# Seven-product weight pairs: second chunk split first, the first unit's copies dealt out, other pairs in units 2 and 3

## The chip, the cores and the metric

The kernel runs on one core of a Trainium2 chip. The metric is the device time of one execution in microseconds (us). The core has five engines, each with its own instruction queue: TensorE (PE in the profile) multiplies matrices into PSUM, VectorE (DVE) and ScalarE (ACT) work on elements, GpSimd (POOL) does some element work and issues accumulating DMAs, SyncE (SP) issues the loads of the weights. Engines wait for one another by semaphores, and each takes its instructions in the order in which they were written to it.

## The reference

The model is a trunk of two layers over 256 tokens of width 2048, all in float32. Layer 0 mixes tokens by attention (16 query heads, 4 key heads), layer 1 by a recurrent block. After each mixer comes a gated feed-forward of width 5632, and this is what the change touches:

```
x = x + mixer(rms_norm(x, norm_mix[i]))
x = x + swiglu(rms_norm(x, norm_ffn[i]), w_gate[i], w_up[i], w_down[i])

def swiglu(h, w_gate, w_up, w_down):
    return (silu(h @ w_gate) * (h @ w_up)) @ w_down
```

## The kernel before, in words

**Precision.** Each float32 weight chunk (128 x 1024) is split in two reduced-precision parts: ACT casts it to "hi" and DVE subtracts, giving "lo". A product of an activation block and a weight block is then three matmuls of 128 x 512: activation hi by weight hi, activation lo by weight hi, activation hi by weight lo (`product`, L323, L324 and L326). The last of the three is the first that needs "lo".

**Units.** The gate and up projections of a feed-forward are cut into 11 units of 512 features (numbered 0 to 10 in the code; the text calls them unit 1 to 11). A unit goes through the 2048 rows of the weights in eight pairs, 0 to 7, of 256 rows. Each pair is two chunks in DRAM: one of the gate weights, one of the up weights, 512 KB each. Within a chunk lie two blocks of 128 rows x 512 features. With the two halves of the tokens, a pair is a 2 x 2 by 2 x 2 block product.

**Plain pairs and seven-product pairs.** A plain pair forms its eight block products (`wide`, 24 matmuls). A seven-product pair forms seven (21 matmuls) from sums of blocks, in the manner of Strassen's and Winograd's scheme. Its weight operands are b11 and b21 (the two blocks of the first chunk), t1 = b11 + b12 and b22 (in the second chunk), t2 = t1 + b22, t3 = t2 - b11 and t4 = b21 + t2. Matching sums of the activations (`Norm.form`) are made once for each feed-forward. `SEVEN` names the pairs treated so in most units, `FEWER` the exceptions in units 1 to 3.

**Preparing a seven-product pair** (`load_seven`, from L149). Two loads land in "raw" tiles. t1 is made in place: on DVE (L174) when the three loads ahead of it are plain ones (`soon`), otherwise by an accumulating DMA that POOL issues (L176) once both chunks have landed. Then the inner function `two` casts a whole chunk on ACT (L163) and subtracts on DVE (L164). `combine` makes t2, t3 and t4 in place in the raw tiles (DVE, L169) and casts them (ACT, L170, "ohi" for t2 and "hi" for t3 and t4), and three remainders follow (DVE, L171, "olo" for t2). In a plain pair `load_half` does the cast (L145) and the remainder (L146).

**Order.** PE's order is written out by hand. The other engines' orders come from a planner that simulates a timeline, with added rules: `behind("cast", ...)` chains all casts on ACT in program order, and `behind("rest", ...)` chains the remainders and sums on DVE. `follow` and `ahead` add single rules of that kind. Buffers limit how far the preparation can run ahead: 8 raw tiles and 7 pairs of hi and lo tiles, of which a seven-product pair takes three.

**The end of a unit.** `sums` (L769 to L773) combines four of the products in PSUM, L791 to L795 add the rest and apply SiLU and the product of gate and up. DVE then transposes 32 x 32 blocks (L408) and 16 small copies (L416, 404 ns each on ACT) move them into place. A cast (L801) and a remainder (L802) make the operand of the down projection. With `beside`, the 16 copies aren't issued at once: they are put in four portions on the list `tail`, the last with L801 and L802, and each following `load_seven` issues one. Without it all 16 follow at once. Before the change unit 1 and the last unit are without it. The tiles "one" and "two" have one buffer each, so a unit's `sums` come after all portions of the unit before it.

**Neighbours.** Units 1 and 2 follow each other directly, then unit 3; from there on two down projections (`wide_project`, plain chunks) stand between units. Unit 1 follows the mixer's output projection, whose last PSUM banks DVE adds to x at L347.

Of the kernel before, what the change touches and what calls it, by code (L numbers as in the profile page):

```python
# [12 lines left out]
F32 = mybir.dt.float32  # L13
F32R = mybir.dt.float32r
AF = mybir.ActivationFunctionType
ALU = mybir.AluOpType
AX = mybir.AxisListType

P = 128
# [8 lines left out]
PARTS = [8, 8, 8, 8, 12]  # L28
UNIT = 4
SEVEN = (0, 1, 2, 4, 5, 6)  # L30
FEWER = {0: (0, 5, 6), 1: (4, 5, 6), 2: (1, 4, 5, 6)}
HALF = 8
CHUNK = HALF * P
WIDE = 512
# [40 lines left out]
def trunk(ctx, tc, w, out):  # L75
    nc = tc.nc
    act, dve, pool, pe, sync = nc.scalar, nc.vector, nc.gpsimd, nc.tensor, nc.sync
# [11 lines left out]
    def nm(s):  # L89
        uid[0] += 1  # L90
        return f"{s}_{uid[0]}"

    def tmp(tag, shape=(P, S), dt=F32, bufs=2):
        pl = tp if tag in COMMON else scope[-1]
        return pl.tile(list(shape), dt, tag=tag, name=nm(tag), bufs=bufs)
# [4 lines left out]
    def follow(i, j):  # L100
        tc.add_manual_dep(
            i.ins, j.ins.name,
            mybir.DependencyInfo(mybir.DependencyClass.NoSync, mybir.DependencyReason.DATA),
            reason="order",
        )
# [12 lines left out]
    def landing(shape):  # L118
        n = used[0] = (used[0] + 1) % (RING + RAWS)
        if ft and n >= RING:  # L120
            return scope[-1].tile(shape, F32, tag="xraw", name=nm("raw"), bufs=RAWS)
        return wp.tile(shape, F32, tag="raw", name=nm("raw"), bufs=RING)

    def behind(key, i):
        if key in newest:
            follow(i, newest[key])
        newest[key] = i
        for rule in [rule for rule in ahead if key == rule[2]]:
            rule[0] -= 1
            if rule[0] == 0:  # L130
                follow(i, rule[1])
                ahead.remove(rule)
# [21 lines left out]
    def load_seven(srcs, soon):  # L154
        raw = [landing([P, 2, WIDE]) for _ in range(2)]
        for r, src in zip(raw, srcs):
            sync.dma_start(out=r, in_=src)
        (b11, b21), (t1, b22) = ([r[:, j, :] for j in range(2)] for r in raw)
        got = {}

        def two(src, names):
            hi, lo = parts([P, 2, WIDE])
            behind("cast", act.copy(hi, src))  # L163
            behind("rest", dve.tensor_tensor(lo, src, hi[:].bitcast(F32), ALU.subtract))  # L164
            for j, name in enumerate(names):
                got[name] = hi[:, j, :], lo[:, j, :]

        def combine(o, x, y, op, hi, lo):
            behind("rest", dve.tensor_tensor(o, x, y, op))  # L169
            behind("cast", act.copy(hi, o))  # L170
            return lambda: behind("rest", dve.tensor_tensor(lo, o, hi.bitcast(F32), ALU.subtract))  # L171

        if soon:
            behind("rest", dve.tensor_tensor(t1, b11, t1, ALU.add))  # L174
        else:
            pool.dma_start(out=t1, in_=b11, accum_op=ALU.add)  # L176
        two(raw[0], ("b11", "b21"))
        two(raw[1], ("t1", "b22"))
        if tail:
            tail.pop(0)()  # L180
        one = [tmp(t, (P, WIDE), F32R) for t in ("ohi", "olo")]
        hi, lo = parts([P, 2, WIDE])
        got["t2"] = tuple(one)
        got["t3"], got["t4"] = ((hi[:, j, :], lo[:, j, :]) for j in range(2))
        t2 = b22
        rests = [
            combine(t2, t1, b22, ALU.add, *got["t2"]),
            combine(b11, t2, b11, ALU.subtract, *got["t3"]),
            combine(b21, t2, b21, ALU.add, *got["t4"]),
        ]  # L190
        while parted:
            follow(parted.pop(), newest["cast"])
        for rest in rests:
            rest()
        return got
# [21 lines left out]
    def ffn_order(l):  # L217
        seq = []
        for what, i in ffn_plan():
# [3 lines left out]
            both = [(w[f"w_gate{l}"][i, c], w[f"w_up{l}"][i, c]) for c in range(KT // 2)]  # L223
            seq += sum(([b] if c in (FEWER.get(i, SEVEN)) else list(b) for c, b in enumerate(both)), [])
        return seq + out_order(w[f"w_down{l}_{len(PARTS) - 1}"], UNIT // 2)
# [524 lines left out]
    def ffn(norm, nxt):  # L750
        def bank():
            return ps_m.tile([P, 2 * S], F32, tag="pm", name=nm("pm"))

        def unit(seven, beside, engines, soon):
            xs, r = norm.xs, [norm.r[:, a : a + 1] for a in range(2)]
            m1, p5, p6, p7 = (bank() for _ in range(4))
            c11, c21, c12, c22 = (new_acc() for _ in range(4))
            new = [m1, p5, p7, p6, c11, c21, c12, c22]

            def fresh(o):  # L760
                n = len(new)
                new[:] = [b for b in new if b is not o]
                return len(new) < n

            one, h = (tmp(n, (P, 2, WIDE), bufs=1) for n in ("one", "two"))
            (base, u), (v, x) = ([t[:, a, :] for a in range(2)] for t in (one, h))

            def sums():
                follow(act.copy(base, m1), newest["cast"])  # L769
                dve.tensor_tensor(u, base, p6, ALU.add)  # L770
                dve.tensor_tensor(v, u, p5, ALU.subtract)
                dve.tensor_tensor(u, u, p7, ALU.add)
                ahead.append([2, dve.tensor_tensor(x, u, p5, ALU.subtract), "rest"])  # L773

            for c in range(KT // 2):
                if c not in seven:
                    for pair in ((c11, c21), (c12, c22)):
                        wide(pair, xs, 2 * c, KT, [fresh(o) for o in pair])
                        if pair[0] is c11 and c == seven[-1] + 1:
                            sums()  # L780
                    continue
                wt, end = half(), c == seven[-1]
                n1, n3, n2, n4 = norm.forms[c]
                a11, a12, a22 = block(xs, 2 * c, 0), block(xs, 2 * c + 1, 0), block(xs, 2 * c + 1, 1)
                for o, y, b in (
                    (m1, a11, "b11"), (c11, a12, "b21"), (p5, n1, "t1"), (c12, n4, "b22"),
                    (p6, n2, "t2"), (p7, n3, "t3"), (c21, a22, "t4"),
                ):
                    product(o, y, wt[b], fresh(o), end and any(o is m for m in (m1, p5, p7, p6)))
            for o, y, b in ((base, base, c11), (u, u, c21)):  # L790
                features = dve.tensor_tensor(o, y, b, ALU.add)  # L791
            for a, (o, y, b) in enumerate(((base, v, c12), (u, x, c22))):
                table_act(o, o, AF.Silu, scale=r[a])
                last = dve.tensor_tensor(y, b, y, ALU.subtract)  # L794
            dve.tensor_tensor(h, h, one, ALU.mult)  # L795
            ahead.extend([[1 if soon else 3, features, "rest"], [2 if soon else 4, last, "rest"]])
            t, ht = act_four(), turn_blocks(h, engines, h, tail if beside else None)

            def whole(move=list):
                move()  # L800
                act.copy(t[:, :, :S], ht)  # L801
                dve.tensor_tensor(t[:, :, S:], ht, t[:, :, :S].bitcast(F32), ALU.subtract)  # L802

            if beside:
                tail.append(partial(whole, tail.pop()))
            else:
                whole()
            return [t[:, k, :] for k in range(UNIT)]

        hid = [[] for _ in PARTS]  # L810
        ends = np.cumsum(PARTS) // UNIT
        for what, i in ffn_plan():
            if what == "unit":
                hid[int(np.searchsorted(ends, i, "right"))] += unit(FEWER.get(i, SEVEN), 0 < i < ends[-1] - 1, (act,) if i < ends[-1] - 1 else (act, dve), i < ends[0])
            else:
                for a, acc in enumerate(wide_project(hid[i[0]], PARTS[i[0]], bank)):
                    t = tmp("form", (P, WIDE))
                    m = act.activation(t, acc, AF.Copy, scale=norm.r[:, a : a + 1])
                    if i[1] % 2:
                        parted.append(m)  # L820
                    pool.dma_start(out=x_tm[:, a, i[1] * WIDE : (i[1] + 1) * WIDE], in_=t, accum_op=ALU.add)
        if nxt is not None:
            ln_exp_tables()
        groups(hid[-1], PARTS[-1], PARTS[-1] - UNIT, lambda: None, partial(add_residual, norm=nxt, store=nxt is None, scale=norm.r))
        scope.pop()
        ft.pop().close()
# [216 lines left out]
```

## Time and profile before

| | |
|---|---|
| median of 3 runs | 1952.77 us (1952.69 to 1953.58) |
| profiled execution | 1952.89 us |
| its span, first to last instruction | 1951.1 us |
| PE busy | 1938.0 us (99%), 9224 matmuls |
| DVE busy | 1768.6 us (91%) |
| ACT busy | 1448.3 us (74%) |
| POOL busy | 401.3 us (21%) |
| loads from HBM | 382.13 MB |
| accumulating DMAs for t1 (L176) / sums on DVE (L174) | 90 / 26 |
| chunks of seven-product pairs (L163) | 232, so 116 pairs |
| first feed-forward's units | 266.39 us to about 884 us |
| second feed-forward's units | 1263.38 us to about 1881 us |

A row of the timeline has the start in us from the start of the span, the duration in us, engine, line, operation, the tile written and the tiles read, shapes and count. In brackets stands how long the engine sat idle ahead of it and what ended that. A matmul's row has a duration that overlaps with the next one's, so its cost has to be read from the distance of two starts.

### The profile page before, as it was taken

Reading aid. Unit: us, or ns where it says so; the run is one execution under the profiler, and the core shown is the slowest. Engines: PE = TensorE matmul, PEld = TensorE weight load, DVE = VectorE, ACT = ScalarE, POOL = GpSimd, SP = SyncE. Lnnn points to the kernel's source line nnn. Section 1 sums busy time; section 2 is a strip of 40 time slices with the busy share of each in tenths; the row PEclk is TensorE's granted clock in tenths of the full one; section 3 lists DMA queues with packets and bytes.
Section 4 is the critical chain, followed back from the end, with each engine's and each line's share of the span. In section 5 each row is a group of like instructions: output and inputs, shape, how many; then the busy total and the mean of one; then the engine's idle time right before and its main releaser. Section 6 shows DMA issues by size and latency. Waiting matters only on the chain.

```text
span 1951.1 us, 27630 instructions
## 1 busy us (share of the span) xinstructions
PE 1938.0 (99%) x9224; PEld 1624.0 (83%) x9224; DVE 1768.6 (91%) x2417; ACT 1448.3 (74%) x2358; POOL 401.3 (21%) x497
## 2 busy tenths in 40 slices
PE   9999999999999999999999999999999999999999
PEld 8898888788888888888899998887888888888887
DVE  7878698999999999998799997898999999999993
ACT  7677686777777777777698887866778776787772
POOL 0442250011101111010465450520101111011100
PEclk9999999999999999999999999999999999999999
DMA  8434746698878978787365556555878888788872
GB/s 328 156 127 152 248 158 197 196 272 236 248 233 243 262 240 246 235 244 246 126 223 188 189 164 245 175 194 174 253 236 248 245 248 253 231 246 251 246 257 86
DMA packets 131727, 426.42 MB, mean 219 GB/s; under 512 B 14720, under 2 KB 14976, under 8 KB 131584
## 3 DMA queue, kind: packets, MB, share of 16 engines
q1 hardware_dynamic: 108944, 383.21, 58.0%
q0 software_dynamic: 22496, 41.43, 11.9%
q8 instruction: 72, 1.18, 0.2%
q14 instruction: 71, 0.58, 0.1%
q10 hardware_dynamic: 144, 0.02, 0.0%
HBM read 382.13 MB, written 2.10 MB: 197 GB/s over the span
## 4 chain that ended last, share of the span: by engine, by line
PE 92%; DVE 4%; ACT 1%; issue 1%; DMA 1%; POOL 0%; SPq 0%; ACTq 0%; DVEq 0%; POOLq 0%
PE acc L326 14%; PE acc L323 14%; PE acc L324 14%; PE pm L326 11%; PE pm L323 11%; PE pm L324 11%; PE acc L294 8%; PE acc L292 4%; PE pm L306 1%; PE pm L307 1%; PE pm L305 1%; DVE lo L146 1%; ACT hi L145 1%; DVE lo L164 0%; DMA raw<-in_w_in_dram 0%
## 5 line engine op out<-in xcount | busy, mean ns | idle before, releaser
L146 DVE TENSOR_TENSOR lo<-raw,hi 128x1024 fp32r<-128x1024 f32 (+1 forms) x474 | 574.5, 1240 | 77.1 <-ACT hi L145 75.3
L145 ACT CAST hi<-raw 128x1024 fp32r<-128x1024 f32 (+1 forms) x474 | 478.4, 1045 | 116.5 <-PE acc L324 72.1
L326 PE MATMUL acc<-lo,xg 128*128 128x512 f32 x744 | 290.9, 391 | 2.0 <-DVE lo L146 1.8
L323 PE MATMUL acc<-hi,xg 128*128 128x512 f32 x744 | 290.0, 390 | 0.0
L324 PE MATMUL acc<-hi,xg 128*128 128x512 f32 x744 | 289.6, 389 | 0.0
L164 DVE TENSOR_TENSOR lo<-raw,hi 128x1024 fp32r<-128x1024 f32 x232 | 275.0, 1217 | 6.5 <-ACT hi L163 3.8
L294 PE MATMUL acc<-xg,hi 128*128 128x512 f32 x832 | 271.7, 397 | 0.6 <-ACT hi L145 0.6
L163 ACT CAST hi<-raw 128x1024 fp32r<-128x1024 f32 x232 | 234.6, 1048 | 41.0 <-issue 14.4
L176 POOL DMA_DIRECT2D raw<-raw x90 | 77.7, 863 | 903.9 <-DVE raw L174 369.5
L323 PE MATMUL pm<-hi,act 128*128 128x512 f32 x512 | 199.2, 389 | 0.0
L324 PE MATMUL pm<-hi,act 128*128 128x512 f32 x512 | 199.2, 389 | 0.0
L326 PE MATMUL pm<-lo,act 128*128 128x512 f32 x512 | 199.2, 389 | 0.0
L416 ACT COPY two<-one 32x256 f32<-32x256 f32 x420 | 169.7, 404 | 24.7 <-DVE one L408 16.5
L292 PEld LDWEIGHTS acc<-xg,lo 128*128 128x128 f32 x832 | 156.3, 188 | 35.4 <-DVE lo L146 2.8
L323 PE MATMUL acc<-hi,act 128*128 128x512 f32 x448 | 174.9, 390 | 0.4 <-DVE two L794 0.4
L326 PE MATMUL acc<-lo,act 128*128 128x512 f32 x448 | 174.4, 389 | 0.0
L324 PE MATMUL acc<-hi,act 128*128 128x512 f32 x448 | 174.4, 389 | 0.0
L292 PE MATMUL acc<-xg,lo 128*128 128x256 f32 x832 | 171.8, 281 | 1.2 <-DVE lo L146 1.2
L326 PEld LDWEIGHTS acc<-lo,xg 128*128 128x128 f32 x744 | 139.7, 188 | 34.1 <-DVE lo L146 5.4
L324 PEld LDWEIGHTS acc<-hi,xg 128*128 128x128 f32 x744 | 139.7, 188 | 29.2
L323 PEld LDWEIGHTS acc<-hi,xg 128*128 128x128 f32 x744 | 139.7, 188 | 28.6
L170 ACT CAST hi<-raw 128x512 fp32r<-128x512 f32 x232 | 137.1, 622 | 32.8 <-DVE raw L169 31.8
(221 smaller groups left out, 3852.1 us busy)
## 6 DMA issues: line engine op xcount, KB each, us to landing
raw<-in_w_gate_dram SPq DMA_DIRECT2D x176, 512.0 KB, 4.6
raw<-in_w_up_dram SPq DMA_DIRECT2D x176, 512.0 KB, 5.5
raw<-in_w_down_dram SPq DMA_DIRECT2D x176, 512.0 KB, 4.4
raw<-in_w_in_dram SPq DMA_DIRECT2D x64, 512.0 KB, 4.4
raw<-raw POOLq DMA_DIRECT2D x90, 256.0 KB, 5.8
raw<-in_w_q_dram SPq DMA_DIRECT2D x32, 512.0 KB, 3.8
raw<-in_w_o_dram SPq DMA_DIRECT2D x32, 512.0 KB, 4.2
x<-form POOLq DMA_DIRECT2D x64, 256.0 KB, 6.7
```

The source lines that it names most:

```text
L145: behind("cast", act.copy(hi[:, sl], raw[:, sl]))
L146: behind("rest", dve.tensor_tensor(lo[:, sl], raw[:, sl], hi[:, sl].bitcast(F32), ALU.subtract))
L163: behind("cast", act.copy(hi, src))
L164: behind("rest", dve.tensor_tensor(lo, src, hi[:].bitcast(F32), ALU.subtract))
L170: behind("cast", act.copy(hi, o))
L176: pool.dma_start(out=t1, in_=b11, accum_op=ALU.add)
L292: pe.matmul(acc[:, S:], w, xs[k][:, :S], start=False, stop=stop)
L294: pe.matmul(acc, w, xs[k], start=(k == 0), stop=stop)
L323: pe.matmul(o, xh, wh, start=start, stop=False)
L324: pe.matmul(o, xl, wh, start=False, stop=False)
L326: pe.matmul(o, xh, wl, start=False, stop=stop)
L416: m = (eng.copy if eng is act else eng.tensor_copy)(to[:, :, :, i, :], of[:, :, :, j, :])
```

## The change

In `load_seven` the second chunk (t1, b22) is cast and split first. The sum t2 is made right behind it, ahead of the cast and remainder of the first chunk (b11, b21). The cast of t2 comes behind the first chunk's cast, and only then the portion of copies from `tail`. On PE the products that use t1 and b22 go first, then those with b11 and b21. Unit 1 gets `beside`, so its 16 copies are dealt out in four portions. Unit 2 has the pairs 2, 4, 5, 6 as seven-product pairs in place of 4, 5, 6; unit 3 has 2, 4, 5, 6 in place of 1, 4, 5, 6. The number of seven-product pairs becomes 118.

```diff
-FEWER = {0: (0, 5, 6), 1: (4, 5, 6), 2: (1, 4, 5, 6)}
+FEWER = {0: (0, 5, 6), 1: (2, 4, 5, 6), 2: (2, 4, 5, 6)}
...
             pool.dma_start(out=t1, in_=b11, accum_op=ALU.add)
+        two(raw[1], ("t1", "b22"))
+        one = [tmp(t, (P, WIDE), F32R) for t in ("ohi", "olo")]
+        t2 = b22
+        behind("rest", dve.tensor_tensor(t2, t1, b22, ALU.add))
         two(raw[0], ("b11", "b21"))
-        two(raw[1], ("t1", "b22"))
+        behind("cast", act.copy(one[0], t2))
         if tail:
             tail.pop(0)()
-        one = [tmp(t, (P, WIDE), F32R) for t in ("ohi", "olo")]
         hi, lo = parts([P, 2, WIDE])
         got["t2"] = tuple(one)
         got["t3"], got["t4"] = ((hi[:, j, :], lo[:, j, :]) for j in range(2))
-        t2 = b22
         rests = [
-            combine(t2, t1, b22, ALU.add, *got["t2"]),
+            lambda: behind("rest", dve.tensor_tensor(one[1], t2, one[0].bitcast(F32), ALU.subtract)),
             combine(b11, t2, b11, ALU.subtract, *got["t3"]),
             combine(b21, t2, b21, ALU.add, *got["t4"]),
         ]
...
                 for o, y, b in (
-                    (m1, a11, "b11"), (c11, a12, "b21"), (p5, n1, "t1"), (c12, n4, "b22"),
+                    (p5, n1, "t1"), (c12, n4, "b22"), (m1, a11, "b11"), (c11, a12, "b21"),
                     (p6, n2, "t2"), (p7, n3, "t3"), (c21, a22, "t4"),
                 ):
...
-                hid[...] += unit(FEWER.get(i, SEVEN), 0 < i < ends[-1] - 1, (act,) if i < ends[-1] - 1 else (act, dve), i < ends[0])
+                hid[...] += unit(FEWER.get(i, SEVEN), i < ends[-1] - 1, (act,) if i < ends[-1] - 1 else (act, dve), i < ends[0])
```

In the last line the index of `hid` is cut.

More of the change, by code (lines that the diff above doesn't have):

```diff
@@ L813, in ffn @@
             if what == "unit":
-                hid[int(np.searchsorted(ends, i, "right"))] += unit(FEWER.get(i, SEVEN), 0 < i < ends[-1] - 1, (act,) if i < ends[-1] - 1 else (act, dve), i < ends[0])
+                hid[int(np.searchsorted(ends, i, "right"))] += unit(FEWER.get(i, SEVEN), i < ends[-1] - 1, (act,) if i < ends[-1] - 1 else (act, dve), i < ends[0])
             else:
```

## The prediction

> **What bounds the kernel now.** I read the page's head first, then TensorE's (PE's) own rows for its pace, then PE counted by stretches, and last the rows of VectorE (DVE) and ScalarE (ACT) where PE falls behind.
>
> ```profile
> span 1951.1 us, 27630 instructions
> PE 1938.0 (99%) x9224; PEld 1624.0 (83%) x9224; DVE 1768.6 (91%) x2417; ACT 1448.3 (74%) x2358; POOL 401.3 (21%) x497
> PE 92%; DVE 4%; ACT 1%; issue 1%; DMA 1%; POOL 0%; SPq 0%; ACTq 0%; DVEq 0%; POOLq 0%
> ```
>
> PE holds 92% of the chain of waits, DVE 4%. The change can gain by fewer matmuls or where PE waits. PE rows at the first feed-forward's start:
>
> ```profile
> 266.39 0.39 PE L323 MATMUL pm<-hi,xg 128*128 128x512 f32 x1
> 266.62 0.39 PE L324 MATMUL pm<-hi,xg 128*128 128x512 f32 x1
> ...
> 267.07 0.39 PE L323 MATMUL acc<-hi,xg 128*128 128x512 f32 x1
> ...
> 267.52 0.39 PE L326 MATMUL acc<-lo,xg 128*128 128x512 f32 x1
> ```
>
> Five steps take 1.13 us: a matmul costs 0.2267 us (rounded times, over longer stretches), though each row says 0.39, since they overlap. So a plain pair (24 matmuls) is 5.44 us of PE, a seven-product pair (21) 4.76.
>
> PE counted by stretches (us, busy and count, clock, DMA share, GB/s):
>
> ```profile
> 270.00:330.00 60.00, 60.00 (x266) 1.00 0.58 184
> ...
> 340.00:356.00 16.00, 15.16 (x65) 1.00 0.63 216
> 356.00:392.00 36.00, 34.67 (x149) 1.00 0.62 194
> ...
> 1337.00:1353.00 16.00, 15.14 (x65) 1.00 0.63 216
> 1353.00:1389.00 36.00, 34.66 (x149) 1.00 0.61 194
> ```
>
> At full pace 60 us hold 60/0.2267 = 264.7, and the count has 1.3 more because it takes in matmuls begun earlier. At that pace 16 us would hold 71.9 and 36 us 160.1. PE is 6.9 and 11.1 short: 1.56 us lost around the end of the second unit, 2.52 us in the third, 4.08 us in each feed-forward and 8.2 us in both. The clock is full, so this is waiting.
>
> Why PE is late there, in ACT's and DVE's rows:
>
> ```profile
> 320.76 6.64 ACT L416 COPY two<-one 32x256 f32<-32x256 f32 x16 [1.11 <-DVE one L408]
> ```
> ```profile
> 308.68 5.76 DVE L146 TENSOR_TENSOR lo<-raw,hi 128x1024 fp32r<-128x1024 f32 x5
> 314.35 1.21 DVE L795 TENSOR_TENSOR two<-two,one 128x1024 f32<-128x1024 f32 x1
> ...
> 317.76 0.68 DVE L174 TENSOR_TENSOR raw<-raw,raw 128x512 f32<-128x512 f32 x1
> ...
> 328.08 0.69 DVE L171 TENSOR_TENSOR olo<-raw,ohi 128x512 fp32r<-128x512 f32 x1 [4.19 <-ACT ohi L170]
> ...
> 337.22 2.35 DVE L164 TENSOR_TENSOR lo<-raw,hi 128x1024 fp32r<-128x1024 f32 x2
> 339.61 0.69 DVE L169 TENSOR_TENSOR raw<-raw 128x512 f32<-128x512 f32 x1
> 340.33 1.29 DVE L169 TENSOR_TENSOR raw<-raw,raw 128x512 f32<-128x512 f32 x2
> 341.55 0.69 DVE L171 TENSOR_TENSOR olo<-raw,ohi 128x512 fp32r<-128x512 f32 x1
> 342.15 1.29 DVE L171 TENSOR_TENSOR lo<-raw,hi 128x512 fp32r<-128x512 f32 x2
> 343.35 1.22 DVE L146 TENSOR_TENSOR lo<-raw,hi 128x1024 fp32r<-128x1024 f32 x1
> ...
> 1325.07 0.69 DVE L171 TENSOR_TENSOR olo<-raw,ohi 128x512 fp32r<-128x512 f32 x1 [4.19 <-ACT ohi L170]
> ```
>
> The first unit's 16 copies run as one block of 6.64 us on ACT, ahead of the cast "ohi", and DVE stands 4.19 us for it, in both feed-forwards. One seven-product pair takes DVE from 337.22 to 343.35, 6.13 us, against PE's 4.76; a plain pair takes two of five chunks in 5.76, 2.30 us, against 5.44. Each seven costs DVE's lead 1.4 us and each plain pair returns 3.1: DVE sets the pace where sevens stand close.
>
> **Part 1, one more seven in the second unit.** Three matmuls fewer in each feed-forward: 3 x 0.2267 = 0.68 us, 1.36 in both. By the 0.39 of the rows it would be 2.34; I take the starts. The Trainium skill (Perfetto Trace Analysis, Tensor Engine Instruction) has a matmul's reported end as an estimate from its size, not an observation; by that rule too the 0.39 is no cost, and the spacing of the starts bears it out.
>
> For DVE the pair costs 6.13 - 2.30 = 3.83 us more. The sum of pair 4 (0.61 of DVE, one step of such rows) leaves for a POOL accumulate, since a seven now stands three loads ahead; pair 2 takes one instead. Nothing in balance in unit 2; in unit 3 one sum is gone.
>
> **Part 2, the first unit's copies dealt out.** Four copies (1.65 us of ACT) go behind each of the four sevens, so DVE's 4.19 us go. With part 1: 3.83 - 4.19 = -0.36 us for DVE up to the end of pair 6 in unit 2. Two things move that. The last portion brings the tile's cast and remainder into pair 6, the latest place; in unit 3 they already lie so:
>
> ```profile
> 383.27 1.05 ACT L801 CAST act<-two 128x1024 fp32r<-128x1024 f32 x1
> 384.23 0.61 ACT L170 CAST ohi<-raw 128x512 fp32r<-128x512 f32 x1
> ```
> ```profile
> 384.46 1.22 DVE L802 TENSOR_TENSOR act<-two,act 128x1024 fp32r<-128x1024 f32 x1
> ```
>
> The remainder's DVE time is only moved, but waiting for the cast can cost up to 1.05 us. The other way, the step from 339.61 to 340.33 (0.72 where its neighbours take 0.61) is third sum waiting for second; with a chunk's remainder between them it goes, 0.11 in four sevens, 0.44. Bounds: -0.80 to +0.69; I take 0, between them, as the cast's row shows it in the line and the transpose needed before the copies is a second thing of that kind. So DVE reaches unit 3 when it does now, PE comes 0.68 us earlier and waits 0.68 us longer: unit 2 gains nothing.
>
> **Part 3, unit 3's first seven from pair 1 to pair 2.**
>
> ```profile
> 352.80 0.68 DVE L174 TENSOR_TENSOR raw<-raw,raw 128x512 f32<-128x512 f32 x1
> ...
> 356.81 1.23 DVE L408 STREAM_TRANSPOSE one<-two 128x1024 f32<-128x1024 f32 x1
> ```
> ```profile
> 358.07 1.65 ACT L416 COPY two<-one 32x256 f32<-32x256 f32 x4 [3.37 <-DVE one L408]
> 359.75 0.62 ACT L170 CAST ohi<-raw 128x512 fp32r<-128x512 f32 x1
> ```
> ```profile
> 351.20 0.50 PE L326 MATMUL acc<-lo,xg 128*128 128x512 f32 x1 [0.84 <-DVE lo L146]
> ...
> 360.42 0.50 PE L323 MATMUL pm<-ohi,fh 128*128 128x512 f32 x1 [1.18 <-ACT ohi L170]
> ```
>
> The chain now is transpose, four copies, "ohi", PE. After: from 352.80 DVE does pair 1 (2.30), the unit's product (1.2), the sum (0.6), transpose (1.2), one remainder (1.15), t2 (0.7): 359.95, with ohi at 360.6. PE, from 351.20, has 21 + 24 + 12 matmuls before it needs it, 12.9 us, 364.1. The 1.18 us are gone with 3.5 to spare; the copies stand behind ohi. I leave 0.8 us of the 2.52 for pairs 6 and 7, where that cast still lies: 1.7 us gained, bounds 0.9 and 2.5.
>
> **Part 4, the order inside every seven.** Same instructions, so its own cost is in its waits. At the first pair of the first unit the second product now writes a bank that the output projection has just filled:
>
> ```profile
> 266.75 0.68 DVE L347 TENSOR_TENSOR x<-x,acc 128x512 f32<-128x512 f32 x1
> ```
>
> It is read until 267.43; the second product comes at 267.07. New wait 0.36 plus a restart of 0.1, or nothing if DVE comes earlier: 0 to 0.5, I take 0.25 in each feed-forward.
>
> Where DVE makes the sum, the second chunk's remainder, now next in line, waits for a cast of 1.05 us on ACT between. The previous unit's product (1.21 at 314.35) lies there to fill it; without it 1.05 us is lost at 12 pairs of each feed-forward, and in units 4 to 11, where it is the first pair, the lead below hides it.
>
> In the other units the second chunk's cast now stands first, and behind it are queued first chunk, ohi, copies. It waits for POOL's accumulate (median 5.8 us to landing), formerly covered by the first chunk's cast of 1.05 us. DVE's lead in units 4 to 11 at its smallest, pair 6:
>
> ```profile
> DMA to landing us min/median/max: 3.3/5.8/8.0
> ```
> ```profile
> 374.65 1.05 ACT L163 CAST hi<-raw 128x1024 fp32r<-128x1024 f32 x1 [0.88 <-DMA raw<-raw]
> ```
> ```profile
> 507.13 0.68 DVE L171 TENSOR_TENSOR olo<-raw,ohi 128x512 fp32r<-128x512 f32 x1
> ```
> ```profile
> 509.81 0.39 PE L326 MATMUL pm<-olo,fh 128*128 128x512 f32 x1
> ```
>
> 507.81 to 509.81: 2.0 us. Lateness up to 2.0 us per unit is hidden by this lead. I put 0.4 us in all; bounds 0 and, at 0.4 for each of 16 units, 6.4. Four more accumulates (90 to 94) on a POOL 21% busy are hidden by the same lead.
>
> **Sum.** 2 x (0 + 1.7 - 0.25) - 0.4 = 2.5 us off. The profiled execution took 1952.89 us, 1.8 around its span; the median is 1952.77, so 1950.3.
>
> **Rivals.** A: DVE is faster than I count. If the planner puts the cast late and the hidden steps count, DVE reaches unit 3 0.8 us earlier; part 3 then brings 2.2 and part 4 costs 0.1: 2 x (0.8 + 2.2 - 0.1) = 5.8, 1947.0. For it: -0.36 before any hole. Against: the cast's row in unit 3. Everything gone would be 8.2 + 1.36 = 9.5, 1943.3.
>
> B: the change doesn't do what it says: DVE's stall only changes its place. Cast and transpose come at their worst, +0.69, and take half of part 3: 2 x (0.85 - 0.69) = 0.3, 1952.5. For it: in unit 2 four sevens leave DVE 1.4 us each behind.
>
> C, slower: the accumulate gates. In pairs 1 and 5 of 16 units the second chunk's cast waits for landing and the whole ACT line stands. Place: "hi" of the second chunk; it decides from 2.0 us lateness in one unit. At 2.4, 0.4 us x 16 = 6.4 less 2.5: 1956.7. For it: 0.88 us of wait already with the cast second; landings reach 8.0. Against: nearly all landings now come before the first cast's turn. The Trainium skill (TensorE: The Clock Gate, Architectural detail) has ACT's and DVE's queues as strict FIFO, which speaks against putting the later operand first; the held cast above agrees, the copies standing behind it.
>
> **Chances.** Forecast 0.46, A 0.22, B 0.20, C 0.12. About 0.2%, 3.9 us, is what a measurement tells from no change: below 1948.9 is faster, above 1956.7 slower. The forecast's own range 1948.9 to 1951.9 and B lie within; A is mostly faster, and the rest of the forecast's lower edge adds 0.02: 0.24. C with B's tail: 0.12. Same 0.64. Range 1946.5 to 1955.0: A's centre with a margin, and part of C.
>
> **What would show it.** 9218 matmuls; 94 accumulates, 24 sums on DVE; copies in fours in the first unit; no 4.19 us before "olo". PE's wait for "ohi" in unit 3 gone (part 3 right); its wait for "lo" at unit 3's first pair as long or longer (part 2 right; shorter is A); a wait of "acc" in the first unit's first pair (part 4). Waits of PE in units 4 to 11 are C, and then the forecast is wrong; so it is if unit 3 still waits for more than 1.5 us.

## The result and the profile after

The changed kernel takes 1975.86 us (median of four runs, 1975.66 to 1977.61) against 1952.85 us before: 1.0119 times as long, 95% interval 1.0102 to 1.0137. It is 23 us slower, and the time lies outside the range given.

The head of the page after, with the engines' busy time and the shares of the chain of waits:

```profile
span 1975.8 us, 27650 instructions
PE 1950.3 (99%) x9218; PEld 1617.2 (82%) x9218; DVE 1783.7 (90%) x2427; ACT 1445.3 (73%) x2364; POOL 407.0 (21%) x501
PE 62%; DVE 17%; ACT 12%; issue 7%; DMA 1%; POOL 0%; ACTq 0%; DVEq 0%; SPq 0%; POOLq 0%
```

The 9218 matmuls are there, six fewer than before, and the granted clock is full as before. PE is still called 99% busy, but its share of the chain fell from 92% to 62%, and DVE and ACT together rose from 5% to 29%. The chain moves between ACT and DVE, and PE waits for them. The busy share did not show this: PE's busy time even grew by 12.3 us, with six matmuls fewer. A matmul's row lasts 0.39 us (0.50 behind a wait) where the next one should start 0.23 us after it, so the first part of each delay lies under the row before.

What PE waited for in the changed kernel (us in total, times, longest):

```profile
PE pm L328 <- DVE olo L189: 5.3, 19, 0.3
PE acc L328 <- DVE lo L146: 4.1, 8, 0.9
PE acc L328 <- DVE lo L171: 2.4, 4, 0.6
PE acc L325 <- DVE two L796: 2.3, 2, 1.1
```

Line 189 is the remainder of t2 ("olo"), the remainder that was L171 before. 19 waits of about 0.3 us stand there; before there was none of this line in the list. They are spread over the units:

```
start of ...             before    after    later by
unit 1, first FF         266.39   266.51     0.12
unit 4                   416.19   418.40     2.21
unit 5                   477.39   481.39     4.00
unit 6                   538.60   543.56     4.96
unit 11                  844.59   856.16    11.57
unit 1, second FF       1263.38  1277.57    14.19
unit 4                  1413.19  1429.16    15.97
unit 11                 1841.59  1864.46    22.87
end of the span          1951.1   1975.8    24.7
```

(FF is a feed-forward; starts in us, PE's first matmul of the unit. The profiled execution after is the slowest of its four, 1977.61 us, so the last row says 24.7 and not 23.) The first three units lose 2.1 and 1.8 us. Most of the loss is made in units 4 to 11, where the kernel before had no wait worth naming: a unit with its two down projections took 61.2 us and now takes 62.17, again and again (62.99 and 63.92 in two pitches of the first feed-forward).

DVE counted over four such pitches, first and last row of each view (us, busy and count, clock, DMA share, GB/s). Before:

```profile
477.39:538.60 61.21, 59.24 (x73) 1.00 0.84 246
...
661.00:722.20 61.20, 59.24 (x73) 1.00 0.83 246
```

After:

```profile
481.39:543.56 62.17, 59.55 (x73) 1.00 0.83 242
...
667.88:730.04 62.16, 58.70 (x72) 1.00 0.81 243
```

Same number of instructions, 0.31 us more busy time, but DVE now stands 2.62 us in a pitch where it stood 1.97. (The last row after is no regular pitch: its end cuts one instruction off, hence 72, and it holds one wait of 0.94 us more, at 728.28, behind a cast that ACT held for an accumulate.) It is slower because it waits, while it has become the engine that sets the pace. Its waits over the four pitches before:

```profile
DVE olo L171 <- ACT ohi L170: 3.6, 4, 0.9
DVE one L791 <- PE acc L326: 0.9, 4, 0.2
DVE act L802 <- ACT act L801: 0.7, 4, 0.2
```

and after:

```profile
DVE lo L171 <- ACT hi L170: 5.6, 4, 1.4
DVE lo L164 <- ACT hi L163: 1.7, 5, 0.9
DVE act L804 <- ACT act L803: 1.0, 4, 0.3
DVE lo L146 <- ACT hi L145: 0.7, 4, 0.2
```

9.0 us against 4.3 behind ACT, 2.25 a pitch against 1.08. To see why, follow one pair. ACT's rows at the same seven-product pair (pair 1 of unit 5), before:

```profile
478.23 0.61 ACT L170 CAST ohi<-raw 128x512 fp32r<-128x512 f32 x1
478.74 1.14 ACT L170 CAST hi<-raw 128x512 fp32r<-128x512 f32 x2
479.78 2.00 ACT L163 CAST hi<-raw 128x1024 fp32r<-128x1024 f32 x2
481.80 1.65 ACT L416 COPY two<-one 32x256 f32<-32x256 f32 x4
```

and after, ACT and then DVE:

```profile
481.64 0.69 ACT L820 ACTIVATE form<-pm,nr 128x512 f32<-128x512 f32 x1 [0.67 <-PE pm L328]
482.23 0.61 ACT L182 CAST ohi<-raw 128x512 fp32r<-128x512 f32 x1
482.86 1.65 ACT L418 COPY two<-one 32x256 f32<-32x256 f32 x4
484.54 1.14 ACT L170 CAST hi<-raw 128x512 fp32r<-128x512 f32 x2
```
```profile
480.62 1.22 DVE L164 TENSOR_TENSOR lo<-raw,hi 128x1024 fp32r<-128x1024 f32 x1
481.87 1.29 DVE L169 TENSOR_TENSOR raw<-raw,raw 128x512 f32<-128x512 f32 x2
483.08 0.69 DVE L189 TENSOR_TENSOR olo<-raw,ohi 128x512 fp32r<-128x512 f32 x1
485.19 1.30 DVE L171 TENSOR_TENSOR lo<-raw,hi 128x512 fp32r<-128x512 f32 x2 [1.42 <-ACT hi L170]
```

Before, the three casts of t2, t3 and t4 follow one another (478.23, 478.74 twice), and the portion of four copies comes after the two whole-chunk casts, ahead of the next pair's "ohi". There ACT had nothing else to do, because "ohi" must wait for DVE to make the sum. After, the portion lies between "ohi" and the casts of t3 and t4. DVE has made t3 and t4 by about 483.1, but their cast starts at 484.54, when the four copies are through, and DVE stands 1.42 us. The sums were not late; the copies had lost the idle time of ACT in which they used to run.

### The profile page after: what moved, and what is told of

Its sections match the earlier page's. It is cut to its first block, busy times and chain, and to the rows that moved or that the text cites. A ratio compares the mean times of both kernels' runs of the same rounds, so it can differ in the third digit from the quotient of the medians.

```text
span 1975.8 us, 27650 instructions
## 1 busy us (share of the span) xinstructions
PE 1950.3 (99%) x9218; PEld 1617.2 (82%) x9218; DVE 1783.7 (90%) x2427; ACT 1445.3 (73%) x2364; POOL 407.0 (21%) x501
## 4 chain that ended last, share of the span: by engine, by line
PE 62%; DVE 17%; ACT 12%; issue 7%; DMA 1%; POOL 0%; ACTq 0%; DVEq 0%; SPq 0%; POOLq 0%
PE acc L328 9%; PE acc L325 9%; PE acc L326 9%; PE acc L296 8%; PE pm L328 7%; DVE lo L164 6%; PE pm L326 6%; PE pm L325 6%; PE acc L294 4%; ACT two L418 4%; DVE lo L146 3%; ACT hi L170 2%; ACT hi L145 2%; ACT ohi L182 2%; DVE raw L180 1%
## 5 line engine op out<-in xcount | busy, mean ns | idle before, releaser
L146 DVE TENSOR_TENSOR lo<-raw,hi 128x1024 fp32r<-128x1024 f32 (+1 forms) x470 | 572.3, 1246 | 77.6 <-ACT hi L145 75.9
L164 DVE TENSOR_TENSOR lo<-raw,hi 128x1024 fp32r<-128x1024 f32 x236 | 287.8, 1220 | 9.1 <-ACT hi L163 7.3
L325 PE MATMUL acc<-hi,xg 128*128 128x512 f32 x732 | 286.2, 391 | 1.0 <-ACT hi L170 1.0
L326 PE MATMUL acc<-hi,xg 128*128 128x512 f32 x732 | 285.3, 390 | 0.0
L294 PEld LDWEIGHTS acc<-xg,lo 128*128 128x128 f32 x832 | 156.1, 188 | 36.1 <-DVE lo L146 3.5
L171 DVE TENSOR_TENSOR lo<-raw,hi 128x512 fp32r<-128x512 f32 x236 | 155.1, 692 | 24.3 <-ACT hi L170 23.9
L294 PE MATMUL acc<-xg,lo 128*128 128x256 f32 x832 | 171.6, 281 | 2.1 <-DVE lo L146 2.1
L182 ACT CAST ohi<-raw 128x512 fp32r<-128x512 f32 x118 | 73.2, 621 | 123.3 <-DVE raw L180 122.1
```

The costliest lines, as they stand in the source:

```text
L146: behind("rest", dve.tensor_tensor(lo[:, sl], raw[:, sl], hi[:, sl].bitcast(F32), ALU.subtract))
L294: pe.matmul(acc[:, S:], w, xs[k][:, :S], start=False, stop=stop)
L325: pe.matmul(o, xh, wh, start=start, stop=False)
L326: pe.matmul(o, xl, wh, start=False, stop=False)
```

## The experiments

Four theories were set against one another. **P**: the place of the portion of copies on ACT; it moved from ahead of "ohi", where ACT stood idle, to behind it. **Q**: the pairs chosen in units 1 to 3 overfill DVE. **R**: PE's new product order needs t1 and b22 too early. **S**: the early second chunk and sum, with the first chunk's remainder now late; the copies are bystanders. Their numbers stand in what was expected of each run.

### The change with the copies ahead of "ohi" again

```diff
         two(raw[0], ("b11", "b21"))
-        behind("cast", act.copy(one[0], t2))
         if tail:
             tail.pop(0)()
+        behind("cast", act.copy(one[0], t2))
```

> The changed kernel with one step moved back: the portion of copies stands ahead of t2's cast on ScalarE again, behind the first chunk's cast. Theory P (place): in units 4 to 11 each pair that has a portion costs VectorE more, 1.53 us in a unit, since the casts of t3 and t4 now stand behind the copies; with the copies ahead of t2's cast that goes, and about 16 us of the 23 come back: 1957, between 1953 and 1961, and no waits of TensorE for 'olo' in units 4 to 11. Theory Q (pairs): the added pair and the dealt-out copies of units 1 to 3 overfill VectorE and its lead never comes back: 1973 to 1978. Theory R (products): TensorE asks for the second chunk too early: 1973 to 1978.

Measured: 1954.56 us (1952.5 to 1957.32, ten runs), 1.001 [1.0, 1.002] of before. One line moved returns 21.3 of the 23 us. PE's longest waits:

```profile
PE acc L328 <- DVE lo L146: 3.4, 4, 0.9
PE acc L294 <- DVE lo L146: 1.2, 2, 0.8
PE pm L328 <- DVE lo L171: 1.1, 2, 0.6
```

The waits for "olo" are gone, and in units 4 to 11 of both feed-forwards PE waits for nothing but 0.2 us at the end of the last, as before. What remains in the feed-forwards lies in units 2 and 3 (the waits at L294 are in the mixers). P holds; S, which left the loss in place, falls.

### The order alone, with the old pairs and the old first unit

```diff
-FEWER = {0: (0, 5, 6), 1: (2, 4, 5, 6), 2: (2, 4, 5, 6)}
+FEWER = {0: (0, 5, 6), 1: (4, 5, 6), 2: (1, 4, 5, 6)}
...
-unit(..., i < ends[-1] - 1, ...)
+unit(..., 0 < i < ends[-1] - 1, ...)
```

> Only the new order inside a seven-product pair (preparation and products); the pairs of units 2 and 3 and the first unit's copies as before the change. Theory P: units 4 to 11 lose about 1 us each as in the changed kernel, units 1 to 3 little: 1969 to 1975. Theory Q: as before the change, 1951 to 1955. Theory R: 1969 to 1975.

Measured: 1976.88 us (1975.16 to 1978.42), 1.0121 [1.0106, 1.0136]. The order alone costs all of it, a little more than P had put (1969 to 1975). Q falls.

### The pairs and the first unit alone, with the old order

```diff
-FEWER = {0: (0, 5, 6), 1: (4, 5, 6), 2: (1, 4, 5, 6)}
+FEWER = {0: (0, 5, 6), 1: (2, 4, 5, 6), 2: (2, 4, 5, 6)}
...
-unit(..., 0 < i < ends[-1] - 1, ...)
+unit(..., i < ends[-1] - 1, ...)
```

> Only the pairs 2, 4, 5, 6 in units 2 and 3 and the first unit's copies dealt out; the order inside a pair as before the change. Theories P and R: units 4 to 11 run as before the change; by the forecast's parts 1 to 3 the time is 1950 to 1953. Theory Q: 1969 to 1978.

Measured: 1950.17 us (1949.1 to 1950.81, ten runs), 0.9984 [0.9974, 0.9993]. This half of the change is a small gain of 2.9 us over the runs of before beside it (1953.06), and the version is faster than both kernels. PE's longest waits in it:

```profile
PE pm L326 <- DVE olo L171: 2.4, 4, 0.6
PE acc L292 <- DVE lo L146: 2.3, 4, 1.1
PE acc L326 <- DVE lo L146: 1.6, 2, 0.8
```

The wait for "ohi" in unit 3 (2.4 us, twice 1.2, before) is no longer in the list; waits for "olo" of 0.6 us at the ends of units 2 and 3 stand in its place.

### The change with the old product order

```diff
-(p5, n1, "t1"), (c12, n4, "b22"), (m1, a11, "b11"), (c11, a12, "b21"),
+(m1, a11, "b11"), (c11, a12, "b21"), (p5, n1, "t1"), (c12, n4, "b22"),
```

> The changed kernel with TensorE's products in the order of before (b11, b21, then t1, b22); the preparation keeps its new order. Theory P: VectorE's time for a pair stays, TensorE's waits for 'olo' stay, 1973 to 1979. Theory R: 1951 to 1957. Theory Q: 1973 to 1979.

Measured: 1979.09 us (1978.2 to 1980.34), 1.0133 [1.0118, 1.0148]. R falls: with the old product order it is 3.2 us above the change, not below (the two intervals overlap, so no more than that can be said). PE's first wait is

```profile
PE pm L328 <- DVE lo L164: 20.6, 21, 1.1
```

Line 164 is the remainder of a whole chunk. With the first chunk's products first again, PE asks for the remainder that this order makes last. The waits only change their place.

### The portion still later: behind the cast of t4

```diff
         behind("cast", act.copy(one[0], t2))
-        if tail:
-            tail.pop(0)()
...
             combine(b21, t2, b21, ALU.add, *got["t4"]),
         ]
+        if tail:
+            tail.pop(0)()
```

> The changed kernel with the portion of copies moved further back, behind t4's cast. Theory P says that what counts is ScalarE's idle time at the place where the portion stands: in the changed kernel ScalarE idles 1.2 us ahead of t2's cast and 1.2 us ahead of t3's, and next to nothing behind t4's cast, where the next pair's first cast follows at once. So each portion of 1.65 us should now delay the next pair by about 1.6 us, 6 to 7 us in each of the 16 units: 2030 to 2080. A rival (theory S: not the place but the early sum and the late first chunk cost the time, with the copies a bystander) says 1973 to 1980, as changed.

Measured: 2074.99 us (two runs), 1.0624 [1.0605, 1.0644]. The portion now lies ahead of the next chunk's whole cast, which DVE needs next. What DVE waited for over the whole span:

```profile
DVE lo L146 <- ACT hi L145: 112.6, 86, 3.3
DVE lo L164 <- ACT hi L163: 90.1, 57, 2.0
```

In the changed kernel the same two were 75.9 and 7.3 us. The kernel is 122 us over the one before with the same copies here, 23 with them where the change has them, 1.5 with them ahead of "ohi".

The time lies in the range that P gave, but not as P worked it out. By the starts of the units, units 4 to 11 lose about 3.5 us each against the changed kernel, not 6 to 7. The rest, 20 us in each feed-forward, is made ahead of unit 4. There PE stood for up to 4.8 us at a time, and behind such stops the granted clock was down for some us (0.54 in 364 to 368, 0.50 in 1472 to 1476), so part of the 122 us is a slower PE and not the copies themselves.

### The kernel before, with only the portion moved behind "ohi"

```diff
         two(raw[1], ("t1", "b22"))
-        if tail:
-            tail.pop(0)()
...
-        rests = [
-            combine(t2, t1, b22, ALU.add, *got["t2"]),
+        rests = [combine(t2, t1, b22, ALU.add, *got["t2"])]
+        if tail:
+            tail.pop(0)()
+        rests += [
```

> The kernel before with one step moved and nothing else: the portion of copies stands between t2's cast and t3's, in the old order of chunks, the old products and the old pairs. Theory P: there ScalarE idles 0.2 us where a portion takes 1.65, so a portion costs VectorE over 1 us in each of four pairs: clearly slower, 1985 to 2040. Theory S: 1951 to 1956.

Measured: 2034.11 us (2031.23 to 2034.56), 1.041 [1.0394, 1.0426]. The place alone is enough, in the old order too. DVE in one pitch, and its largest wait over four of them:

```profile
461.47:526.41 64.94, 59.51 (x73) 1.00 0.78 231
```
```profile
DVE lo L171 <- ACT hi L170: 17.2, 16, 1.2
```

That is four waits in each pitch, one for each pair with a portion, of 1.08 us. It can be followed in the rows above. Behind t2's sum DVE has two more sums and "olo", 1.3 + 0.7 = 2.0 us, before it needs the cast of t3; ACT has "ohi", the portion and that cast, 0.6 + 1.65 + 0.6 = 2.85, so DVE is 0.85 short by the durations alone. In the change the whole first chunk's remainder (1.22) stands on DVE's side too, 3.2 us against 2.85, which is why the change loses much less: its wait shows where "ohi" itself comes late, at pair 1 behind the down projection's "form" (481.64 above).

The pitch explains 16 x 3.73 = 60 of the 81 us. Most of the rest is made once in each feed-forward, at about 400 and 1437 us: PE stood 4.8 us at once, and the granted clock behind it was 0.50 in 404 to 408 and in 1440 to 1444.

### Two portions at once

The version with the pairs and the first unit alone, with a second portion given out at pair 2 of units 2 and 3 (`sevens` counts the seven-product pairs, 59 in a feed-forward):

```diff
         if tail:
             tail.pop(0)()
+            if sevens[0] % 59 in (3, 7):
+                tail.pop(0)()
+        sevens[0] += 1
```

> The pairs and the dealt-out copies alone, in the old order (the run before of this kind), and two portions instead of one at pair 2 of units 2 and 3, so that the last portion with the operand's cast and remainder falls in pair 5 and not in pair 6. If the operand's cast ahead of t2's cast in pair 6 is what remains of the waits there (1.0 us at the end of units 2 and 3 in each feed-forward, less what the units' end needs), two to three us come back: 1946.5 to 1949. If VectorE's sheer load is what remains, no change: 1949.5 to 1951.

Measured: 1956.76 us (1956.38 to 1957.36, eleven runs), 1.002 [1.0011, 1.0029]. Both expectations missed: it is 6.6 us slower than without the second portion, 1.7 us in each of units 2 and 3 of both feed-forwards by the starts of the units. ACT and DVE at one of these four places:

```profile
317.67 2.49 ACT L421 COPY two<-one 32x256 f32<-32x256 f32 x6
320.18 0.62 ACT L172 CAST ohi<-raw 128x512 fp32r<-128x512 f32 x1
```
```profile
320.83 0.69 DVE L173 TENSOR_TENSOR olo<-raw,ohi 128x512 fp32r<-128x512 f32 x1 [2.14 <-ACT ohi L172]
```

The place ahead of "ohi" has room for one portion (1.65 us), not for eight copies (3.3 us). Beyond it the copies hold "ohi", and DVE stands 2.14 us. The expectations had counted the copies as free at that place, whatever their number.

### The copies ahead of "ohi", with the old product order

```diff
-        behind("cast", act.copy(one[0], t2))
         if tail:
             tail.pop(0)()
+        behind("cast", act.copy(one[0], t2))
...
-(p5, n1, "t1"), (c12, n4, "b22"), (m1, a11, "b11"), (c11, a12, "b21"),
+(m1, a11, "b11"), (c11, a12, "b21"), (p5, n1, "t1"), (c12, n4, "b22"),
```

> The changed kernel with the copies ahead of t2's cast (the first run) and TensorE's products in the old order, first chunk first. The first chunk's remainder is made 1.75 us later than before the change while TensorE asks for it first, so if VectorE's lead of 2 to 3 us in pair 6 is enough the time is 1953 to 1957, and if not, units 4 to 11 show waits for the first chunk's 'lo': 1957 to 1970.

Measured: 1952.78 us (1951.87 to 1954.42, ten runs), 0.9999 [0.999, 1.0008]. That is 0.2 us below the first range, and its reason holds: PE's list has waits for the first chunk's remainder at two places only (0.6 us in all, in unit 2) and none in units 4 to 11. No version with the second chunk first reached the 1950.17 us of the old order. In the profiled executions this one is 2.6 us over the pairs alone, but hardly by its order: one wait in the second layer's mixer, at 1007.66, takes 2.2 us of it.

### How much lateness DVE can hide in a unit

The kernel before, with one of the remainders of t2 made twice in the first two pairs of each unit from the fourth on, then in the first three (`nth` counts the seven-product pairs from unit 4 of a feed-forward on). This adds 0.61 us of DVE work each time and writes the same values again:

```diff
+        nth = sevens[0] % 58 - 10
+        sevens[0] += 1
+        if nth >= 0 and nth % 6 < 2:
+            rests[0]()
         for rest in rests:
             rest()
```

> The kernel before, with the second sum's remainder (olo) made twice in the first two pairs of every unit from the fourth to the eleventh: two more DVE instructions of 128x512 in each of 16 units, a step of 0.61 us each, 1.2 us per unit, none of them later than the other work needs. It measures what DVE has to spare in a unit. Budget theory (DVE stands 1.96 us in a pitch of 61.2 us, but most of that behind ACT's casts; what the changed kernel lost, 0.97 us of 1.53, leaves some 0.6 us to spare): 0.6 x 16 = 10 us slower, 1958 to 1966. If all of the 1.96 us are to spare, or the lead of 2.0 us covers each unit anew, as the prediction had it: hidden, 1952 to 1954.

> The same with the remainder made twice in the first three pairs of every unit from the fourth on: 1.8 us of DVE more per unit. Budget theory with 0.6 us to spare: 1.2 x 16 = 19 us slower, 1967 to 1977, and 9 to 10 us above the run with two, a slope of one. If all of the 1.96 us are to spare, or the lead of 2.0 us covers each unit anew: still hidden, 1952 to 1955.

Measured: 1955.5 us (1954.42 to 1957.59, ten runs), 1.0015 [1.0006, 1.0025] with two; 1962.21 us (1961.27 to 1962.96, four runs), 1.0047 [1.003, 1.0064] with three. Both expectations from the budget theory were too high (1958 to 1966, 1967 to 1977), and those of full cover too low. DVE in one pitch with two,

```profile
477.39:538.60 61.21, 60.56 (x75) 1.00 0.83 246
```

and with three:

```profile
448.32:509.96 61.64, 60.95 (x76) 1.00 0.82 243
```

With two, DVE is busy 60.56 of 61.21 us, and units 4 to 11 of both feed-forwards take as long as before. The profiled execution, the slowest of the ten (1957.59), loses most of its time in the second layer's mixer, by one wait at 1009 us and a granted clock of 0.53 and 0.62 in the 4 us from there, which the profile of the kernel before did not have:

```profile
PE acc L300 <- DVE act L387: 2.0, 1, 2.0
```

The version of the section before has the same wait (2.2 us) without any repeats. With three the pitch is longer by 0.43, which is 6.9 us in 16 units, and the run with three is 6.7 us above the run with two. So DVE can fill a pitch until some 0.7 us of idle time is left (0.65 with two, 61.64 - 60.95 = 0.69 with three). The kernel before had 61.21 - 59.24 - 0.69 = 1.28 us to spare in every unit. Its largest wait, 0.9 us for "ohi" at pair 1, was no loss: a DVE that comes later finds "ohi" ready, and with two repeats only 0.2 us of it is left in four pitches.

This can be held against the change by its waits, without using its pitch. In the rows of a regular pitch DVE stands 1.42 + 0.17 + 0.25 + 0.18 = 2.02 us behind ACT; with three repeats 0.18 remains. So 1.84 us of waiting and 0.31 us of work came on top, 1.28 us of it could be hidden, and 0.87 should show. The pitch grew by 0.96. The same sum for the run with only the portion moved (waits of 17.2 + 2.2 + 0.7 us in four pitches, 0.27 us of work) gives 0.27 + 5.03 - 0.18 - 1.28 = 3.84, and its pitch grew by 3.73.

The sum takes it that a wait of the new kind can't be filled as the old one was. The chain of what released what in the changed kernel, in its next unit (start, duration), shows why this is likely:

```profile
543.81 0.69 ACT form L820
544.50 0.51 ACT ohi L182
545.03 0.40 ACT two L418
...
546.71 1.14 ACT hi L170 x2
...
548.84 1.24 DVE lo L164
...
576.48 0.50 PE pm L328
```

PE's last matmul of the down projection (543.50) releases "form"; "ohi", the copies and the casts follow on ACT without a break; DVE stands for them; and at pair 6 PE waits for DVE's "olo". A late DVE makes PE late, PE ends the next down projection late, and the same line on ACT starts late: the wait is carried along. The smaller waits (0.17 to 0.25 us) begin with DVE's own sum and are carried in the same way. Added work in the changed kernel, which would test this, was not tried.

## Why the prediction was wrong, point by point

**Part 1, one more seven in unit 2: right.** 9218 matmuls, 94 accumulates and 24 sums on DVE, as said; a matmul costs 0.2267 us by the starts. The 0.68 us are lost again at the end of unit 2, as part 2 said.

**Part 2, the first unit's copies: nearly right.** DVE's 4.19 us are gone: in the version with the pairs alone the wait is 0.5. Unit 2 was to gain nothing. PE there, from 340 to 356, holds 62 matmuls where it held 65:

```profile
340.00:356.00 16.00, 14.57 (x62) 1.00 0.59 189
356.00:392.00 36.00, 35.41 (x155) 1.00 0.70 215
```

Three more are lost around the end of unit 2, 0.7 us, as the working expected.

**Part 3, unit 3's first seven at pair 2: right, a little oversized.** The second row has 155 matmuls against 149, 6 x 0.2267 = 1.4 us, where 1.7 was put. Parts 1 to 3 came to 2 x 1.7 = 3.4 us off, 1949.4; alone they give 1950.17.

**Part 4, the order inside every seven: here it failed.** The step was "Same instructions, so its own cost is in its waits", followed by a search for these waits that looked at the new wait for a bank, at the second chunk's cast and at POOL's accumulate, and put 0.4 us in all, bounded at 0.4 in each of 16 units. The portion of copies was not costed as a step that moved, though the diff shows it going from ahead of t2's cast to behind it. The working even names the move twice: part 3 counts it as a help ("the copies stand behind ohi"), and part 4 lists "first chunk, ohi, copies". Neither asks what stands behind the copies. Its price is in the rows of before that were already on the table: four copies at 404 ns behind one another, ahead of two casts that DVE needs within 2.0 to 3.2 us. The other terms came out so:

- The cast behind a sum that DVE makes itself cost nothing, as the working said: the last unit's product and transpose lie in between (594.41 to 596.83 us, ahead of the first remainder of the next unit).
- The wait for a bank at the first pair of unit 1, put at 0.25 us: it did not come. The second product starts 0.68 us after the first, without a break.

```profile
266.51 0.39 PE L325 MATMUL pm<-hi,fh 128*128 128x512 f32 x1
...
267.19 0.39 PE L325 MATMUL acc<-hi,fh 128*128 128x512 f32 x1
```

- A wait that was not forecast came at the first pair of unit 2, and in the version with the copies ahead as well (a step of 1.33 us at 308.82), so it is the new order's and not the copies':

```profile
309.74 0.50 PE L328 MATMUL acc<-lo,xg 128*128 128x512 f32 x1 [0.94 <-DVE lo L146]
```

- "Lateness up to 2.0 us per unit is hidden by this lead" took a lead at one place for a cover that comes back in every unit. What comes back is what DVE has to spare in a pitch, 1.28 us by the runs with repeats: DVE is busy 91% of the span, but 97% of units 4 to 11 (59.24 of 61.21 us). The lateness was 0.31 + 1.84 = 2.15 us a unit, so nearly 1 us of it came through in each of 16 units, where 0.4 us in all was put.

**The rivals.** C forecast the right side, and the sign named for it, PE's waits in units 4 to 11, is what came. Its mechanism is not what happened: in units 4 to 11 the second chunk's cast waited for an accumulate only once in the first feed-forward (0.8 us) and not at all in the second. It was the copies in ACT's line; C's price was 1956.7 and what came lies four times as far from the forecast (25.6 us against 6.4). A and B both rested on units 1 to 3 and never came into play. The rule quoted beside C did bear on the change, only at another instruction. The Trainium skill ("TensorE: Matmul & The Clock Gate", Architectural detail) has ACT's queue as strict FIFO; the rows of after agree, with the casts of t3 and t4 held until 484.54 behind the copies from 482.86. Under that rule the question to ask of each moved ACT instruction is what stands behind it.

**What stays open.** The order with the copies ahead (1954.56) is 4.4 us over the version with the pairs alone, and its runs spread over 4.8 us. Its profiled execution, the fastest of the ten, shows 1.7 us of that, among it the wait at 308.82 and its like at 1306.69; the rest has no row. Two other versions show a wait of 2.0 and 2.2 us in the second layer's mixer; whether the slower executions of this one have it too is not on record. In the first feed-forward one unit of the changed kernel lost 2.7 us rather than 0.96; ACT stood there for a buffer that an accumulate to x still read:

```profile
732.04 0.69 ACT L820 ACTIVATE form<-pm,nr 128x512 f32<-128x512 f32 x1 [2.27 <-DMA x<-form]
```

Whether the new order made that transfer late was not tried.

## What to carry to other kernels

Filler work on an in-order engine is free only at the place where that engine waits for something else, and only up to the length of that wait. When a diff moves a line, list every instruction that changes its neighbours, the small ones too, and ask what is queued behind each and when the next engine needs it. Judge the spare time of an engine in the repeating stretch, not over the span, and ask of each wait whether a late engine would fill it or carry it along.

## What was not expected

- The same four copies (1.65 us) on the same engine left the new order 1.5, 23 or 122 us over the kernel before, by their place within one pair's casts, and the old order 0 or 81 us (122 and 81 with some us of a lower granted clock in them).
- DVE filled 60.56 of 61.21 us with work of many short instructions and still held up nobody; 1.2 us of added work per unit, 19 us over the 16 units, cost nothing in the units, while the changed kernel lost 0.96 us a unit with 59.55 us of work.
